# Splitting an operand one step behind its addition, and giving the chunk products of the RWKV key projection all four quarters of the TensorE array

## Chip, core and metric

The kernel runs on one core of a Trainium2 chip. The metric is the device time of one execution in microseconds (us). TensorE is PE in the views, its weight loads PEld, VectorE DVE, ScalarE ACT, GpSimd POOL, and SP the engine whose queue issues most DMAs.

## What is computed

Two decoder layers over 2048 tokens of width 1024: a sliding-window attention layer, then an RWKV-7 time-mixing layer, each followed by a gated per-layer embedding. The change touches only the RWKV layer. Cut to what matters:

```python
def rwkv7_mixer(h, mu, w_in, ...):
    xx = jnp.pad(h, ((0, 0), (1, 0), (0, 0)))[:, :-1] - h
    xs = h[None] + xx[None] * mu[:, None, None, :]          # token-shifted operands, one per projection
    proj = jnp.einsum('cbtd,dce->cbte', xs[:4], w_in.reshape(C, 4, RWKV_WIDTH))
    r, k, v, z = proj[0], proj[1], proj[2], proj[3]
    ...
    def step(S, inp):                                       # 16 heads of 64 x 64 state, 2048 steps
        sa = jnp.einsum('bhvk,bhk->bhv', S, -kk_t)
        S = S * d_t[:, :, None, :] + sa[..., None] * (kk_t * a_t)[:, :, None, :] + v_t[..., None] * k_t[:, :, None, :]
        y = jnp.einsum('bhvk,bhk->bhv', S, r_t)
        return S, y
```

The kernel does the recurrence in chunks of 64 tokens. Inside a chunk the steps are tied together by a 64 x 64 triangular matrix for each head, which has to be inverted. Its entries are products of decayed keys with each other; the projection phase computes them and leaves them in DRAM, and the recurrence phase reads them and inverts them.

## The kernel before

Four phases follow each other: `attn_proj` (to about 780 us), `attention` (to about 1215), `rwkv_proj` (to about 1960) and `rwkv` (to the end). Float32 matrices are multiplied in three passes: `split` (L531 to L540) makes a rounded high part with a ScalarE copy (L538) and a low part with a subtraction (L540, on VectorE or GpSimd), and `mm3` (L589 to L591) issues high x high, high x low, low x high. A projection tile of 128 channels x 512 tokens is 8 steps k of 3 matmuls of 128x512, 24 in all.

`rwkv_proj` computes r, then k, then v. For each it walks over 4 pairs of channel tiles and, in a pair, over 4 groups n of 512 tokens. Two kinds of generators run beside the projections, advanced by one `tick` per k step:

- `fill(c, n)` makes the operand of projection c for token group n: for each of 8 steps it loads `hp`, ScalarE scales it into `xs` (L974), VectorE adds the shifted part (L975), and `split` makes `xH` and `xL` from `xs`. `xs` has 2 buffers, `hp` 3.
- `evac_r`, `evac_k`, `evac_v` take a finished tile out of PSUM. `evac_k`, 32 times in all, is the long one: low-rank product `ls` (L1029), its tanh `lth` (L1031), squares split into `sh` and `so`, head sums `ss` (L994, L995), a VectorE transpose of `ss` (L1060), a reciprocal root on GpSimd, then the operands `kee` and `kx`, and at last the product `pab` (L1092): for each of 8 chunks and for both heads of the tile one 64x64 matmul. `pab` is copied to `kab` (L1095), two 32-row blocks are moved inside it (L1099), and it goes to DRAM.

The array's rows are the partitions that a matmul reads, its columns those that it writes. A 64x64 matmul takes a quarter of the array: head e reads partition half e, and in the kernel before writes half e, so `pab` uses two of the four quarters, and one PSUM tile.

`ls`, `ss` and `pab` share a PSUM pool `p_s` of 3 buffers, one bank each, in the order in which the program claims them; a fourth claim waits until the tile three claims back has been read. In `evac_k` there are three claims: `ls`, `ss`, `pab`. The other 5 of the 8 banks hold projection tiles.

The order on each engine is not that of the Python code. The tile framework runs a list scheduler over the recorded instructions with a timing model of its own and fixes a queue for each engine; on the chip each engine takes its queue strictly in that order and waits on semaphores.

In the last phase, `chain(c)` runs for each of 32 chunks: `r1p` (L1350), `up` (L1370, rows of one half, columns of the same half for each head), `y` (L1362) and the turned output `ytp` (L1365). `y` of head h reads and writes half h of its bank, `ytp` reads half h and writes the other half in another bank; the two are issued alternately.

## Time and profile before

| | us |
|---|---|
| median of 3 runs (3050.54 to 3063.81) | 3053.57 |
| the profiled execution | 3054.03 |
| its span, first to last instruction | 3052.3 |
| PE busy | 2828.1 (93%) |
| DVE busy | 1888.7 (62%) |
| ACT busy | 1341.6 (44%) |
| mean granted clock of TensorE | 0.965 |

A view by stage tells more than these shares: the r projection with its fills is about 1215 to 1395, the k projection with `evac_k` about 1440 to 1770, and fills for k and v lie at about 1398 to 1493 and 1654 to 1769. A wait view lists, for PE, which tile it waited to use, who released it, total us, how often, and the longest. In a timeline row stand start, duration, engine, line, operation, tiles and count; equal neighbours are merged. Matmuls overlap in the pipeline, so the cost of one is the distance of starts, not its duration. A float32 matmul of 64x64 has two records, so `pab` with its 16 matmuls is 32 records.

### The profile page before, as it was taken

To read this page: it belongs to the slowest core of one execution; us is meant where nothing else is said; L and a number is where in the kernel's file an instruction comes from. 1 tells how busy PE (TensorE), PEld (TensorE's weight loads), DVE (VectorE), ACT (ScalarE), POOL (GpSimd) and SP (SyncE) were. 2 spreads that over 40 slices of the span, in tenths; PEclk is the share of its full clock that TensorE was granted. 3 is DMA by queue.
4 is the path that set the end of the run, shared out by engine and by line. 5 is a ranking of instruction groups with operands and counts; after the bars stand their busy time and mean duration, and the time that the engine had idled before them with its cause. 6 is when DMAs were issued, how large, how long until landed. Compare 5 with 4: busy or idle time off the path is not lost. (4 is left out here: it accounts for less than half of the span.)

```text
span 3052.3 us, 56599 instructions
## 1 busy us (share of the span) xinstructions
PE 2828.1 (93%) x21416; PEld 2241.3 (73%) x21416; DVE 1888.7 (62%) x3433; ACT 1341.6 (44%) x2872; POOL 1006.4 (33%) x886
## 2 busy tenths in 40 slices
PE   7999999899999999799899899888889889889987
PEld 5888887677777777587677678666767677677866
DVE  6532434676677655747777876686684785774444
ACT  5311114784465543525768743333334344334422
POOL 2242510001221242303656610224454435435421
PEclk9999999999999999999999999999899999999999
DMA  7664857999887587636656788887879889759674
GB/s 224 189 143 104 167 146 219 285 284 337 271 257 218 196 276 253 176 128 179 199 186 206 217 218 219 243 283 190 203 195 240 219 224 253 181 164 260 186 252 159
DMA packets 625232, 652.43 MB, mean 214 GB/s; under 512 B 261696, under 2 KB 435904, under 8 KB 624960
## 3 DMA queue, kind: packets, MB, share of 16 engines
q1 hardware_dynamic: 617280, 638.32, 70.7%
q0 software_dynamic: 7680, 10.50, 3.1%
q8 instruction: 169, 2.77, 0.4%
q14 instruction: 103, 0.84, 0.1%
HBM read 421.40 MB, written 216.79 MB: 209 GB/s over the span
## 5 line engine op out<-in xcount | busy, mean ns | idle before, releaser
L589 PE MATMUL ps<-dhi,dwh 128*128 128x512 f32 x1472 | 609.0, 415 | 37.4 <-ACT dhi L538 17.7
L591 PE MATMUL ps<-dhi,dwl 128*128 128x512 f32 x1472 | 589.8, 401 | 12.8 <-DVE dwl L536 8.3
L590 PE MATMUL ps<-dlo,dwh 128*128 128x512 f32 x1472 | 592.0, 403 | 7.4 <-DVE dlo L540 4.7
L589 PE MATMUL ps<-xH,wh 128*128 128x512 f32 x1408 | 551.2, 398 | 17.1 <-ACT xH L538 11.7
L590 PE MATMUL ps<-xL,wh 128*128 128x512 f32 x1408 | 556.1, 395 | 7.4 <-DVE xL L540 4.2
L591 PE MATMUL ps<-xH,wl 128*128 128x512 f32 x1408 | 556.0, 395 | 5.5 <-DVE wl L540 5.5
L589 PEld LDWEIGHTS ps<-dhi,dwh 128*128 128x128 f32 x1472 | 281.9, 192 | 110.6 <-ACT dhi L538 20.2
L591 PEld LDWEIGHTS ps<-dhi,dwl 128*128 128x128 f32 x1472 | 282.2, 192 | 79.3 <-DVE dwl L536 9.2
L590 PEld LDWEIGHTS ps<-dlo,dwh 128*128 128x128 f32 x1472 | 282.4, 192 | 65.7 <-DVE dlo L540 6.6
L589 PEld LDWEIGHTS ps<-xH,wh 128*128 128x128 f32 x1408 | 265.1, 190 | 81.0 <-ACT xH L538 17.1
L590 PEld LDWEIGHTS ps<-xL,wh 128*128 128x128 f32 x1408 | 266.7, 189 | 70.1 <-DVE xL L540 7.2
L591 PEld LDWEIGHTS ps<-xH,wl 128*128 128x128 f32 x1408 | 266.7, 189 | 64.4 <-DVE wl L540 7.9
L699 POOL DMA_DIRECT2D t<-t x160 | 126.2, 1256 | 201.3 <-issue 79.2
L873 ACT ACTIVATE S<-S,nm 128x256 f32<-128x256 f32 (+1 forms) x256 | 125.5, 492 | 67.0 <-DVE nm L870 60.5
L540 POOL TENSOR_TENSOR xL<-xs,xH 128x512 fp32r<-128x512 f32 x72 | 103.4, 1443 | 110.0 <-ACT xH L538 104.8
L538 ACT ACTIVATE wh<-wr 128x1024 fp32r<-128x1024 f32 x44 | 46.6, 1059 | 185.3 <-DMA wr<-in_attn_w_in 151.5
L864 DVE CUSTOM_DVE_ANT_0 S<-sc,mask,sink 128x256 f32<-128x256 f32 (+1 forms) x256 | 108.8, 469 | 25.7 <-PE sc L860 25.6
L1285 DVE TENSOR_TENSOR tmp<-P 128x30 f32<-128x30 f32 (+14 forms) x240 | 111.0, 462 | 11.5 <-POOL P L1276 5.0
L975 DVE SCALAR_TENSOR_TENSOR xs<-hp,mu,xs 128x512 f32<-128x512 f32 x96 | 82.0, 861 | 47.2 <-ACT xs L974 41.6
L1287 DVE TENSOR_TENSOR P<-P,tmp 128x30 f32<-128x30 f32 (+14 forms) x240 | 105.9, 441 | 6.8
L540 POOL TENSOR_TENSOR dlo<-z,dhi 128x512 fp32r<-128x512 f32 x16 | 22.3, 1411 | 262.1 <-ACT dhi L538 255.5
L540 POOL TENSOR_TENSOR so<-sq,sh 128x512 fp32r<-128x512 f32 x32 | 45.1, 1408 | 189.2 <-ACT sh L538 123.4
(258 smaller groups left out, 5288.2 us busy)
## 6 DMA issues: line engine op xcount, KB each, us to landing
hp<-hn SPq DMA_DIRECT2D x72, 256.5 KB, 3.9
sz<-th SPq DMA_DIRECT2D x64, 256.0 KB, 4.6
ple<-pt SPq DMA_DIRECT2D x64, 256.0 KB, 6.9
aux<-ple SPq DMA_DIRECT2D x64, 256.0 KB, 4.5
yd<-kx SPq DMA_DIRECT2D x32, 512.0 KB, 4.4
dwh<-wp_ao SPq DMA_DIRECT2D x24, 512.0 KB, 4.7
dwl<-wp_ao SPq DMA_DIRECT2D x24, 512.0 KB, 6.0
dwh<-wp_ag SPq DMA_DIRECT2D x24, 512.0 KB, 4.3
```

The lines of the kernel that those rows point to most:

```text
L538: nc.scalar.activation(hi, src, AF.Copy)
L540: e.tensor_tensor(out=lo, in0=src, in1=f32(hi), op=ALU.subtract)
L589: mm(ps, lhsT=wh, rhs=ah, start=first, stop=False)
L590: mm(ps, lhsT=wh, rhs=al, start=False, stop=False)
L591: mm(ps, lhsT=wl, rhs=ah, start=False, stop=last)
L699: nc.gpsimd.dma_start(out=t1[32 * d:32 * d + 32, :], in_=t2[32 * a:32 * a + 32, :], accum_op=ALU.add)
L864: nc.vector.tensor_tensor_reduce(out=S[:, i, c0:], in0=sc[:, eo, c0:], in1=mask[:, c0:], scale=1.0, scalar=sink[:, 4 * g + 2 * j + eo:4 * ...
L873: nc.scalar.activation(S[:, i, c0:], S[:, i, c0:], AF.Exp, bias=nm[:, i:i + 1], accum_out=den[:, i:i + 1])
L975: nc.vector.scalar_tensor_tensor(out=src, in0=t[:, :G], scalar=mus[:, c, k:k + 1], in1=src, op0=ALU.mult, op1=ALU.add)
L1285: nc.vector.tensor_tensor(out=t, in0=P[:, 0:r, r:r + 1].broadcast_to([128, r, n]), in1=P[:, r:r + 1, r + 1:].broadcast_to([128, r, n]), op ...
L1287: nc.vector.tensor_tensor(out=P[:, 0:r, r + 1:], in0=P[:, 0:r, r + 1:], in1=t, op=ALU.add)
```

## The change

In `fill`, the split of step k - 1 is written ahead of the scaling and the addition of step k, where it stood behind the addition of its own step; the number of ticks per fill stays 16 at the usual pace. In `evac_k`, even chunks go to one PSUM tile and odd chunks to a second one, and in odd chunks the two heads write the opposite halves, so all four quarters of the array are addressed. `pab` now makes two claims on `p_s`, four in all for `evac_k`. The copy to `kab` becomes two copies of half the size, and the block moves read `kab` instead of PSUM. Since the halves of odd chunks are now swapped in DRAM, `chain` writes `r1p` of odd chunks into swapped halves and reads `tt` and `r1` from there; `up` of an odd chunk reads one half and writes the other.

```diff
--- before.py
+++ after.py
@@ -965,17 +965,20 @@
                     nc.sync.dma_start(out=t[:, n == 0:], in_=hn1[rows, n * G - (n > 0):n * G + G])
                     return t
 
-                ts = [load(0), load(1)]
-                for k in range(KT):
+
+                ts, src = [load(0), load(1)], None
+                for k in range(KT + 1):
                     if k + 2 < KT:
                         ts.append(load(k + 2))
                     yield
-                    t, src = ts[k], fp.tile([128, G], F32, name="xs", bufs=2)
-                    nc.scalar.activation(src, t[:, 1:], AF.Copy, scale=omu[:, c, k:k + 1])
-                    nc.vector.scalar_tensor_tensor(out=src, in0=t[:, :G], scalar=mus[:, c, k:k + 1], in1=src,
-                                                   op0=ALU.mult, op1=ALU.add)
-                    self.split(H[n, k], L[n, k], src, lo_engine="pool" if k % 4 else "dve")
-                    for _ in range(pace - 1):
+                    if k:
+                        self.split(H[n, k - 1], L[n, k - 1], src, lo_engine="pool" if k % 4 != 1 else "dve")
+                    if k < KT:
+                        t, src = ts[k], fp.tile([128, G], F32, name="xs", bufs=2)
+                        nc.scalar.activation(src, t[:, 1:], AF.Copy, scale=omu[:, c, k:k + 1])
+                        nc.vector.scalar_tensor_tensor(out=src, in0=t[:, :G], scalar=mus[:, c, k:k + 1], in1=src,
+                                                       op0=ALU.mult, op1=ALU.add)
+                    for _ in range(pace - 1 if 0 < k < KT else 0):
                         yield
 
             def proj(ps, w, n):
@@ -1086,17 +1089,20 @@
                 for _ in range(12):
                     yield
 
-                pab = p_s.tile([128, G], F32, name="pab", tag="s")
+
+                pab = [p_s.tile([128, G // 128, 64], F32, name="pab", tag="s") for _ in range(2)]
+                h = (slice(0, 64), slice(64, 128))
                 for c in range(G // 64):
-                    for h in (slice(0, 64), slice(64, 128)):
-                        nc.tensor.matmul(pab[h, c * 64:c * 64 + 64], lhsT=x[h, c, 0], rhs=ee[h, c * 64:c * 64 + 64],
+                    for e in range(2):
+                        nc.tensor.matmul(pab[c % 2][h[e ^ (c % 2)], c // 2], lhsT=x[h[e], c, 0], rhs=ee[h[e], c * 64:c * 64 + 64],
                                          start=True, stop=True)
                 ao = ring("d", "kab")
-                nc.scalar.copy(ao, pab)
+                for o in range(2):
+                    nc.scalar.copy(ao.rearrange("p (c o t) -> p o c t", o=2, t=64)[:, o], pab[o])
 
                 for e in range(2):
-                    v, u = (x[64 * e + 32:64 * e + 64].rearrange("p (c t) -> p c t", t=64) for x in (ao, pab))
-                    nc.scalar.copy(v[:, :, 0:32], u[:, :, 32:64])
+                    v = ao[64 * e + 32:64 * e + 64].rearrange("p (c t) -> p c t", t=64)
+                    nc.scalar.copy(v[:, :, 0:32], v[:, :, 32:64])
                 nc.sync.dma_start(out=ab[rc], in_=ao)
 
             def evac_v(ps, ct, n):
@@ -1347,7 +1353,7 @@
                 pairs = [(p, eo) for p in range(NP) for eo in range(2)]
                 r1p = p_c.tile([128, NP, 64], F32, name="r1p", tag="ch")
                 for p, eo in pairs:
-                    mm(r1p[half[eo], p], lhsT=am[:, p, eo, 0:LC], rhs=uv[:, eo, p], start=True, stop=True)
+                    mm(r1p[half[eo ^ c % 2], p], lhsT=am[:, p, eo, 0:LC], rhs=uv[:, eo, p], start=True, stop=True)
                 r1 = r2.tile([128, NP, 64], F32, name="r1")
                 nc.scalar.copy(r1, r1p)
                 if c + 1 < NCH:
@@ -1367,7 +1373,8 @@
                     YT[c - 1] = tp
                 up = p_c.tile([128, NP, 64], F32, name="up", tag="ch")
                 for p, eo in pairs:
-                    mm(up[half[eo], p], lhsT=tt[half[eo], p], rhs=r1[half[eo], p], start=True, stop=True)
+
+                    mm(up[half[eo], p], lhsT=tt[half[eo ^ c % 2], p], rhs=r1[half[eo ^ c % 2], p], start=True, stop=True)
                 for eo in range(2):
                     nc.scalar.copy(uv[half[eo], eo], up[half[eo]])
                 self.ticks(STEPS[1])
```

The order on ScalarE in the middle of the r projection, where the fill of token group 2 runs (L974 scales, L538 makes the high part, L1031 and L1042 belong to `evac_r`), before:

```order
L974 ACTIVATE xs<-hp,omu 128x512 x2
L538 ACTIVATE xH_11467<-xs 128x512
L538 ACTIVATE xH_11469<-xs 128x512
L974 ACTIVATE xs<-hp,omu 128x512 x2
L538 ACTIVATE xH_11471<-xs 128x512
L538 ACTIVATE xH_11473<-xs 128x512
L1042 ACTIVATE re<-lth 128x512
L974 ACTIVATE xs<-hp,omu 128x512
L1031 ACTIVATE lth<-ls,v_w_1127 128x512
```

Scalings already stood in pairs here, with the pair of high parts behind the pair of scalings. The same place in the changed kernel, where L978 is the scaling and L1034 and L1045 are the two of `evac_r`:

```order
L978 ACTIVATE xs<-hp,omu 128x512 x2
L538 ACTIVATE xH_11467<-xs 128x512
L538 ACTIVATE xH_11469<-xs 128x512
L978 ACTIVATE xs<-hp,omu 128x512 x2
L538 ACTIVATE xH_11471<-xs 128x512
L538 ACTIVATE xH_11473<-xs 128x512
L1045 ACTIVATE re<-lth 128x512
L978 ACTIVATE xs<-hp,omu 128x512
L1034 ACTIVATE lth<-ls,v_w_1127 128x512
```

Nothing moved but line numbers. The same holds for every row of every engine's queue when the `fill` edit is made alone: the queues, their waits and the tiles' places in memory stay as they were.

The order on PE in the k projection, at one `evac_k` (the eleventh), before:

```order
L590 MATMUL ps_14370<-xL32_11476,wh_13772 128x512
L591 MATMUL ps_14370<-xH32_11475,wl_13773 128x512
L1092 MATMUL pab_14296<-kee_14162,kx_14173 64x64 x16
L994 MATMUL ss_14350<-sh_14283,blk_r_1148 128x512
L995 MATMUL ss_14350<-so_14284,blk_r_1148 128x512
L589 MATMUL ps_14370<-xH33_11477,wh_13772 128x512
L590 MATMUL ps_14370<-xL33_11478,wh_13772 128x512
```

Here `pab` is one piece of 16 matmuls, followed by the head sums of a later tile. The same `evac_k` in the changed kernel (`pab_14316` takes the even chunks, `pab_14317` the odd ones):

```order
L1032 MATMUL ls_14293<-low_14051,l2h_13826 128x512
L1032 MATMUL ls_14293<-low_14051,l2l_13827 128x512
L1097 MATMUL pab_14316<-kee_14180,kx_14191 64x64 x8
L590 MATMUL ps_14392<-xL33_11478,wh_13780 128x512
L591 MATMUL ps_14392<-xH33_11477,wl_13781 128x512
L589 MATMUL ps_14392<-xH34_11479,wh_13780 128x512
L590 MATMUL ps_14392<-xL34_11480,wh_13780 128x512
L591 MATMUL ps_14392<-xH34_11479,wl_13781 128x512
L1097 MATMUL pab_14317<-kee_14180,kx_14191 64x64 x8
L589 MATMUL ps_14392<-xH35_11481,wh_13780 128x512
```

The product is cut in two pieces of 8, with five projection matmuls between; each piece uses two quarters of the array.

The order on PE at the ninth `evac_k` of the changed kernel (before, it was one piece of 16 as above):

```order
L589 MATMUL ps_14220<-xH27_11469,wh_13780 128x512
L1097 MATMUL pab_14144<-kee_14008,kx_14019 64x64 x2
L1097 MATMUL pab_14145<-kee_14008,kx_14019 64x64 x2
L1097 MATMUL pab_14144<-kee_14008,kx_14019 64x64 x2
L1097 MATMUL pab_14145<-kee_14008,kx_14019 64x64 x2
L1097 MATMUL pab_14144<-kee_14008,kx_14019 64x64 x2
L1097 MATMUL pab_14145<-kee_14008,kx_14019 64x64 x2
L1097 MATMUL pab_14144<-kee_14008,kx_14019 64x64 x2
L1097 MATMUL pab_14145<-kee_14008,kx_14019 64x64 x2
L997 MATMUL ss_14200<-sh_14131,blk_r_1148 128x512
L998 MATMUL ss_14200<-so_14132,blk_r_1148 128x512
```

Here the two tiles alternate by chunk, so four matmuls in a row stand in four quarters.

## Rows read from the trace of the kernel before

**Rows 1.** Busy time of each engine by stage of `rwkv_proj`, us:

```profile
core 0: us, PE busy (x) PEld busy (x) DVE busy (x) ACT busy (x) POOL busy (x), PEclk, DMA share, GB/s
1215.00:1395.00 180.00, 162.33 (x671) 124.59 (x670) 97.63 (x117) 71.91 (x112) 34.10 (x47) 0.99 0.49 150
1395.00:1500.00 105.00, 93.84 (x477) 73.40 (x475) 82.10 (x104) 71.84 (x122) 56.08 (x50) 1.00 0.62 181
1500.00:1650.00 150.00, 143.07 (x1074) 112.59 (x1075) 109.67 (x171) 105.70 (x189) 89.91 (x56) 0.98 0.62 202
1650.00:1775.00 125.00, 112.47 (x760) 86.72 (x759) 107.88 (x152) 100.69 (x179) 79.13 (x58) 0.96 0.73 221
```

**Rows 2.** Waits of PE, r projection, 1215 to 1395: us in total, times, longest us:

```profile
PE ps L589 <- ACT xH L538: 8.7, 7, 1.9
PE ps L590 <- DVE xL L540: 3.3, 3, 1.4
```

**Rows 3.** Waits of PE in the k projection, 1395 to 1775:

```profile
PE ss L994 <- ACT sh L538: 10.7, 7, 3.2
PE ss L995 <- DVE so L540: 6.6, 6, 3.0
PE pab L1092 <- DVE kb L1060: 0.3, 1, 0.3
```

**Rows 4.** Timeline of PE at one whole `pab`: start, us, engine, line, tiles:

```profile
1602.04 0.39 PE L590 MATMUL ps<-xL,wh 128*128 128x512 f32 x1
1602.27 0.39 PE L591 MATMUL ps<-xH,wl 128*128 128x512 f32 x1
1602.59 1.15 PE L1092 MATMUL pab<-kee,kx 64*64 64x64 f32 x32
...
1604.01 0.40 PE L995 MATMUL ss<-so,blk_r 128*128 128x512 f32 x1
```

**Rows 5.** Timeline of PE at a `pab` that another matmul cuts in two:

```profile
1594.56 0.40 PE L1029 MATMUL ls<-low,l2h 128*128 128x512 f32 x1
1594.89 0.44 PE L1092 MATMUL pab<-kee,kx 64*64 64x64 f32 x6
1595.26 0.50 PE L1029 MATMUL ls<-low,l2l 128*128 128x512 f32 x1
1595.69 1.02 PE L1092 MATMUL pab<-kee,kx 64*64 64x64 f32 x26
...
1596.98 0.39 PE L995 MATMUL ss<-so,blk_r 128*128 128x512 f32 x1
```

**Rows 6.** Timeline of PE in the last phase, `ytp` and `y` by turns:

```profile
2205.26 0.22 PE L1365 MATMUL ytp<-ident,yc 64*64 64x64 f32 x1
2205.26 0.22 PE L1362 MATMUL y<-uv,xa 64*64 64x64 f32 x1
2205.27 0.22 PE L1365 MATMUL ytp<-ident,yc 64*64 64x64 f32 x1
2205.27 0.22 PE L1362 MATMUL y<-uv,xa 64*64 64x64 f32 x1
2205.32 0.22 PE L1365 MATMUL ytp<-ident,yc 64*64 64x64 f32 x1
```

**Rows 7.** Durations of the copies of `pab`: min/median/max ns:

```profile
L1099 ACT COPY kab<-pab x64: 363/365/371, 1490.3 to 1767.7; 32x256 f32<-32x256 f32 x64
L1095 ACT COPY kab<-pab x32: 567/582/592, 1488.2 to 1764.7; 128x512 f32<-128x512 f32 x32
```

**Rows 8.** Timeline: head sums on PE and their transpose, first and last of 32:

```profile
1459.39 0.40 PE L995 MATMUL ss<-so,blk_r 128*128 128x512 f32 x1
...
1465.94 0.71 DVE L1060 STREAM_TRANSPOSE kb<-ss 128x512 f32<-128x512 f32 x1
...
1731.30 0.40 PE L995 MATMUL ss<-so,blk_r 128*128 128x512 f32 x1
...
1734.58 0.67 DVE L1060 STREAM_TRANSPOSE kb<-ss 128x512 f32<-128x512 f32 x1
```

## Prediction

> **What bounds the kernel now.** I read the stages first. In all of them PE is the busiest engine. In the r projection it works 162.3 of 180 us, in the three stretches of the k projection 93.8 of 105, 143.1 of 150 and 112.5 of 125 [rows 1]. So a microsecond of PE's work counts wherever PE does not wait, and the idle rest (17.7, 11.2, 6.9 and 12.5 us) is what better overlap could return. Then I read the waits. In the r projection PE waits for the high and low parts of the operand, 8.7 and 3.3 us [rows 2]; that is the stall at which the `fill` edit points. In the k projection it waits for the split of the squares, 10.7 and 6.6 us; for a PSUM buffer for `pab` it waits 0.3 us in 36 pieces [rows 3]. Last comes the timeline around one `pab`, because the second edit changes PE's own work there [rows 4 to 6].
>
> **Part 1, `fill`.** No instruction is added or removed. The order shown for ScalarE is the same before and after, and it is the same in every row of every queue when this edit is made alone: the list scheduler had already put two scalings ahead of two high parts. The 12.0 us of waits [rows 2] lie in queues that do not change. Cost 0, gain 0; no cover is needed, since not one DMA or wait moves.
>
> **Part 2, the array's time for `pab`.** A step of the projection is 0.227 us (1602.04 to 1602.27). From the L591 ahead of a whole `pab` to the L995 behind it 1.74 us pass; two ordinary steps take 0.45 of it, so `pab` costs 1.29 [rows 4]. In the last phase `ytp` and `y` address four quarters: four records start within 0.01 us, and the next turn begins 0.058 us later [rows 6]. `pab` has 32 records in two quarters, so 16 turns or 0.93 us; the remaining 0.35 is what entering and leaving costs. With four quarters it would be 8 turns, 0.47 us.
>
> But the gain needs the right order. I counted PE's queue of the changed kernel. Of 32 products 19 stay whole: 7 alternate between the two tiles from the first matmul (0.47 us saved each), 4 after one or two extra pairs (0.35), 2 later still (0.23), and 6 stand as eight even, then about eight odd (0.12, where the two groups overlap). That is 3.3 + 1.4 + 0.5 + 0.7 = 5.9 us. Thirteen are cut in pieces. Twelve of them are 8 and 8, nothing saved (one of these has its first matmul apart as well, 0.1 lost), one is 11 and 5 (0.35 saved). In all **6.1 us of array time go**.
>
> **Part 3, more pieces.** Before, the queue holds 36 pieces of `pab` (28 whole, 4 cut in two), now 46. Each piece pays entering and leaving again: 10 x 0.35 = **+3.5 us**. The other bound is a measured cut: 2.42 us from the L1029 ahead of it to L995, less three steps, is 1.74, against 1.29 whole, 0.45 more [rows 5]; so +4.5 at most. I take 0.35, because most pieces now stand 4 to 20 matmuls apart and not one.
>
> **Part 4, the ring of three banks.** `evac_k` now claims four buffers of three, so a `pab` tile more often has to wait until VectorE has transposed the `ss` of a later tile (L1060). Behind a waiting `pab` the whole PE queue stands: projections, `ss`, `ls`. In the queue before, 22 products wait for such a transpose, with 5.4 to 8.2 us of PE's work between that `ss` and the `pab`; now 26 tiles do, with 1.6 to 6.2 us. The transposes ended 6.9 us after their L995 at the first and 3.6 at the last of 32, on average 3.1 [rows 8]. Each of the 26 distances against each of the 32 lags gives 13.6 us of waits; the same sum for the 22 distances before gives 1.65, and there the row says 0.3 [rows 3], since a PE that waits lets VectorE catch up. A fifth of 13.6 is 2.5; I take **+3 us**. Ends: +12 (13.6 - 1.65), and -5, because the 17.3 us of waits for the squares [rows 3] are dealt out anew and could also fall by a third.
>
> **Part 5, ScalarE.** One copy of 582 ns becomes two of half the size. No copy of 128x256 from PSUM stands here; the move of 32x256 takes 365 ns [rows 7], the nearest row, with as many elements in each partition; I take that: 2 x 0.365 - 0.582 = +0.15 us, 32 times, 4.7 us of ScalarE's time. It is covered where ScalarE is busy 70% (105.7 of 150), hardly where it is busy 81% beside a fill (100.7 of 125) [rows 1] and PE waits for it. A third of the products lie there: **+1 us**, between 0 and 4.7. The two moves now read SBUF; the nearest row is their own 365 ns, so 0.
>
> **Part 6, the recurrence.** `r1p` only swaps halves: 0. `up` of the 16 odd chunks now starts in the two quarters in which the last `ytp` ran, so its first matmuls stand behind two turns: 16 x 0.117 = 1.9 us at most. PE is not always what is waited for there; **+1 us**. The scheduler also shifts single groups of three matmuls in this phase; I give that 0, with 3 us to both sides.
>
> **Sum.** 3054.0 (the profiled execution; the median of the runs is 0.5 lower) - 6.1 + 3.5 + 3 + 1 + 1 = 3056.4. What a measurement can tell from no change is about 0.5%, 15.3 us: below 3038.3 or above 3068.8. Neither edit gets near it.
>
> **Rivals.**
>
> *Ring-bound, slower.* The second tile's wait becomes the rule. PE idles 10% in the stretch where its queue is irregular (12.5 of 125) and 4.6% where it repeats (6.9 of 150) [rows 1]; now the queue is irregular throughout. If the quiet stretch goes to 10% (+8 us) and the two others idle half as much again (+12), the time is 3054.0 - 2.6 + 2 + 20 = 3073. It decides if the transpose regularly lags more than about 4.7 us, the middle of the new distances, instead of 3.1. For it: the first of the 32 lags was 6.9 [rows 8]. Against: 0.3 us of such waits so far.
>
> *Waits for the squares go, faster.* `pab`'s bank is free after copies of about 0.37 us instead of 1.31 (0.582 + 2 x 0.365 [rows 7]), so later claims come earlier and PE has other work to put ahead. Without the 17.3 us: 3054.0 - 2.6 + 2 - 17.3 = 3036. Against: those waits end with ScalarE and VectorE, whose work does not shrink.
>
> *Order does not matter, all 32 products halve.* 32 x 0.47 = 14.9 us saved, +3.5 as above with parts 4 to 6: 3047.6; with no price for the extra pieces 3044. Against: in the turns of rows 6 starts follow the queue, and PE would have to take a later odd chunk ahead of an even one. The Trainium skill ("TensorE: Matmul & The Clock Gate", Part 3) says that matmuls start and end in program order and only weight loads are pulled ahead, which is against this rival too.
>
> *Two tiles give nothing.* If two heads, from different rows, could not write one bank together, a pair of one chunk would run one after the other, and four quarters would be no faster than two: 3056.4 + 6.1 = 3062.5. Against: two of the four records that start within 0.01 us are `y` of both heads, in one bank [rows 6]. The Trainium skill ("TensorEngine Tiling (Array Packing)", Restrictions and Gotchas) states just that limit, that different row tiles cannot access the same bank at the same time; rows 6 disagree, at least for different partition halves.
>
> *The `fill` edit does act.* Then 12.0 us of waits [rows 2] could go: 3044. Against: identical queues.
>
> **How the numbers follow.** Forecast 0.69, ring-bound 0.13, squares 0.05, all halve 0.06, two tiles give nothing 0.05, `fill` acts 0.02. Predicted 3056. The range takes the forecast's bounds: down -6.1 + 3.5 - 5 - 3 is 3043.4, up -6.1 + 4.5 + 12 + 4.7 + 1.9 is 3071; all ends at once are unlikely, so 3045 to 3070. It holds the forecast, most of "halve" and "nothing", and the lower part of ring-bound. Faster by over 0.5% takes the squares and a little of the others, 0.06; slower takes most of ring-bound, 0.12; the rest, 0.82, is within 0.5%.
>
> **What would show it.** After the change, the waits for `xH` and `xL` in the r projection should stay near 12 us (part 1). Whole alternating products should take about 0.8 us between their neighbours less two steps, the cut ones 1.6 together (parts 2, 3). `pab` should show waits of 1 to 5 us in total on the transpose (part 4); over 12 means ring-bound. The two copies should take about 0.37 us each (part 5). I am wrong if the stretch from 1395 to 1775 changes by over 10 us, or if the r projection moves at all.

## The result and the profile after

The changed kernel is slower: 3079.93 us (median of 9 runs, 3068.89 to 3085.27) against 3053.26 (9 runs, 3048.35 to 3063.81); ratio 1.008, 95% interval 1.0068 to 1.0093. Forecast was 3056, between 3045 and 3070. The profiled execution of after has a span of 3076.2 us, that of before 3052.3. So the change costs 0.8%, and the time lies above the range.

Where the 23.9 us lie is read from PE's busy time in stretches that begin and end at the same work in both kernels: from the end of VectorE's last read of an r tile to the last `pab` (the k projection), from there to the first `aps`, the first product of the recurrence phase (the v projection), and from there to the last `ytp` (the recurrence). Columns: stretch, its length, PE busy (records), granted clock, DMA share, GB/s. Before:

```profile
1456.00:1760.00 304.00, 280.19 (x2012) 0.97 0.64 203
1760.00:1956.80 196.80, 187.06 (x864) 1.00 0.84 217
1956.80:2916.50 959.70, 862.76 (x11405) 0.93 0.80 218
```

After:

```profile
1454.30:1781.50 327.20, 288.89 (x2028) 0.95 0.61 193
1781.50:1971.20 189.70, 182.59 (x846) 0.99 0.82 217
1971.20:2941.20 970.00, 867.80 (x11405) 0.92 0.78 216
```

The k projection is 23.2 us longer, the v projection 7.1 shorter (part of its steps now run earlier: 16 records more in the k stretch), together +16.1. The recurrence is 10.3 longer. What comes ahead of the k projection is 1.7 us shorter, what comes behind the recurrence 0.8.

In the k projection PE idles 38.3 us instead of 23.8 (length less busy), 14.5 more. The busy time grew too, by 8.7. Of that 3.6 are the 16 steps that came over from v, at 0.227 us each. The rest is there although the product's own work shrank: the granted clock fell from 0.97 to 0.95, that is, it stood at 1.2 instead of 2.4 GHz for a larger part of the stretch. 0.03 of 304.0 and 0.05 of 327.2 are 9.1 and 16.4 us of full-speed time, so an estimate of what the clock takes is 7 us.

The stages of [rows 1] in the changed kernel, same columns:

```profile
1215.00:1395.00 180.00, 163.31 (x671) 125.42 (x670) 99.84 (x119) 72.89 (x113) 34.12 (x48) 0.98 0.49 150
1395.00:1500.00 105.00, 94.29 (x473) 74.19 (x471) 79.19 (x102) 70.35 (x120) 56.76 (x50) 0.97 0.63 184
1500.00:1650.00 150.00, 136.65 (x1041) 104.98 (x1031) 103.72 (x162) 103.10 (x197) 82.12 (x53) 0.98 0.59 190
1650.00:1775.00 125.00, 105.43 (x682) 80.52 (x683) 107.99 (x148) 100.22 (x189) 83.48 (x59) 0.90 0.66 206
```

The r projection works as before, and the first stretch of k idles as before; the loss begins in the quiet stretch from 1500, idle 13.4 instead of 6.9, and goes on in the next, 19.6 instead of 12.5.

What PE waits for in the k projection, 1395 to 1790, before (the rows that [rows 3] left out):

```profile
PE ps L589 <- DVE kb L1083: 4.4, 6, 1.5
...
PE ss L994 <- ACT kab L1099: 0.7, 2, 0.4
```

and after:

```profile
PE ps L589 <- DVE kb L1086: 18.0, 12, 4.2
PE ss L997 <- ACT kab L1101: 11.3, 6, 3.6
...
PE pab L1097 <- DVE kb L1063: 3.3, 3, 2.2
PE ss L997 <- ACT sh L538: 2.9, 2, 1.9
PE ss L998 <- DVE so L540: 2.1, 2, 1.5
```

The wait that I had priced, `pab` on the transpose, is 3.3 us, just as forecast. Two others grew. `ss` waits for a bank in which a product still lies uncopied (0.7 before, 11.3 now), and a projection waits for one of its five banks until VectorE has made `kb` (4.4 before, 18.0 now). The waits for the squares fell from 17.3 [rows 3] to 5.0.

The two belong together, as the other engines' waits in the same window show. First VectorE and GpSimd of before, then the two and ScalarE of after:

```profile
DVE kb L1060 <- PE ss L995: 2.5, 2, 2.1
...
POOL kb L1064 <- DVE kb L1063: 12.2, 9, 2.9
```

```profile
DVE kb L1063 <- PE ss L998: 10.4, 6, 3.5
...
POOL kb L1067 <- DVE kb L1066: 39.1, 17, 5.0
...
ACT kab L1101 <- PE pab L1097: 10.4, 8, 2.2
```

A late `ss` makes its transpose late, that the root on GpSimd, that `kb`; and `kb` is the last reader of the projection's bank. The starts in the two traces show this for all 32 tiles: from the last matmul of a k tile to its `ss` 15.7 us pass before and 22.0 after, to the end of `kb` 32.3 and 37.3 (means). The fifth tile behind, which needs the bank again, begins 3.5 us after `kb` before and 1.0 after, the first 30 tiles taken. But most of that delay isn't waiting. In PE's queue `ss` stands 40 projection matmuls behind its tile before and 56 after: 16 steps of 0.227 us are 3.7 of the 6.3 us. The scheduler, laying out four claims on three banks, had moved the head sums back before the kernel ran; standing there, they hardly wait for the squares any more.

One place where `ss` does wait, on the timeline of after (start, duration, engine, line; in brackets the idle time ahead and its releaser):

```profile
1546.56 0.98 PE L1097 MATMUL pab<-kee,kx 64*64 64x64 f32 x32
...
1548.23 0.80 ACT L1081 ACTIVATE kb<-lth,oka,v_k_a 128x512 f32<-128x512 f32 x1
1549.03 0.65 ACT L1101 COPY kab<-pab 128x256 f32<-128x256 f32 x2
...
1549.45 0.50 PE L997 MATMUL ss<-sh,blk_r 128*128 128x512 f32 x1 [1.91 <-ACT kab L1101]
...
1550.98 0.63 PE L590 MATMUL ps<-xL,wh 128*128 128x512 f32 x1
...
1551.41 0.63 PE L591 MATMUL ps<-xH,wl 128*128 128x512 f32 x1
```

The product is done by 1547.5, but ScalarE has other work ahead of its two copies and begins them at 1549.03. `ss` needs the bank of one of the two tiles and stands at the head of PE's queue. And after the stall the projection's steps start 0.43 us apart (1550.98, 1551.41) and not 0.23. The granted clock (the column behind the records) was at its upper level through the stall and at its lower one for much of the time behind it:

```profile
1546.00:1549.40 3.40, 1.54 (x35) 1.00 0.20 77
1551.00:1556.00 5.00, 5.00 (x18) 0.71 0.67 157
```

A stall can be paid a second time in this way. Not each one is: PE waits 1.89 us ahead of the L589 at 1599.85 too, and the steps behind that (1600.18, 1600.41) start 0.23 apart. The Trainium skill ("TensorE: Matmul & The Clock Gate", Part 1, "A second HAM failure mode: psum-queue depth-cycling") describes a kernel in which short idle gaps between matmul groups, as it cycles through PSUM banks, make the clock swing between its two levels. The place at 1549.45 agrees with it, 1.00 and then 0.71; the place at 1599.85 does not show it.

### The profile page after: what moved, and what is told of

It is laid out like the page before. It is cut to its first block, busy times and chain, and to the rows that moved or that the text cites. A ratio compares the mean times of both kernels' runs of the same rounds, so it can differ in the third digit from the quotient of the medians.

```text
span 3076.2 us, 56576 instructions
## 1 busy us (share of the span) xinstructions
PE 2838.8 (92%) x21416; PEld 2251.6 (73%) x21416; DVE 1893.0 (62%) x3433; ACT 1345.1 (44%) x2904; POOL 1008.6 (33%) x886
## 5 line engine op out<-in xcount | busy, mean ns | idle before, releaser
L589 PE MATMUL ps<-dhi,dwh 128*128 128x512 f32 x1472 | 608.9, 415 | 27.0 <-ACT dhi L538 9.6
L589 PE MATMUL ps<-xH,wh 128*128 128x512 f32 x1408 | 558.2, 403 | 31.0 <-DVE kb L1086 18.0
L590 PE MATMUL ps<-xL,wh 128*128 128x512 f32 x1408 | 563.4, 401 | 7.5 <-DVE xL L540 4.7
L591 PE MATMUL ps<-xH,wl 128*128 128x512 f32 x1408 | 562.7, 400 | 5.0 <-DVE wl L540 5.0
L589 PEld LDWEIGHTS ps<-dhi,dwh 128*128 128x128 f32 x1472 | 282.1, 192 | 99.7 <-ACT dhi L538 12.4
L589 PEld LDWEIGHTS ps<-xH,wh 128*128 128x128 f32 x1408 | 268.5, 192 | 95.6 <-DVE kb L1086 22.3
L538 ACT ACTIVATE wh<-wr 128x1024 fp32r<-128x1024 f32 x44 | 46.6, 1059 | 177.5 <-DMA wr<-in_attn_w_in 143.3
L864 DVE CUSTOM_DVE_ANT_0 S<-sc,mask,sink 128x256 f32<-128x256 f32 (+1 forms) x256 | 108.9, 470 | 22.2 <-PE sc L860 22.0
L1067 POOL TENSOR_TENSOR kb<-kb,mhalf 128x16 f32<-128x16 f32 x32 | 104.7, 3272 | 41.1 <-DVE kb L1066 39.1
L1291 DVE TENSOR_TENSOR tmp<-P 128x30 f32<-128x30 f32 (+14 forms) x240 | 109.4, 456 | 12.3 <-POOL P L1282 6.2
L264 DVE TENSOR_TENSOR aux<-ps,aux 128x512 f32<-128x512 f32 x64 | 43.8, 686 | 106.6 <-PE ps L591 97.9
```

The lines of the kernel that those rows point to most:

```text
L538: nc.scalar.activation(hi, src, AF.Copy)
L589: mm(ps, lhsT=wh, rhs=ah, start=first, stop=False)
L590: mm(ps, lhsT=wh, rhs=al, start=False, stop=False)
L591: mm(ps, lhsT=wl, rhs=ah, start=False, stop=last)
L864: nc.vector.tensor_tensor_reduce(out=S[:, i, c0:], in0=sc[:, eo, c0:], in1=mask[:, c0:], scale=1.0, scalar=sink[:, 4 * g + 2 * j + eo:4 * ...
L1067: nc.gpsimd.tensor_tensor(out=bs[:, :, 0], in0=bs[:, :, 0], in1=self.mhalf.broadcast_to([128, m]), op=ALU.pow)
```

## Experiments

Each kernel was timed beside the kernel before on the same chip; that one's medians were 3056.44 (e1 to e4), 3055.32 (e5 to e8), 3053.39 (e9 to e12) and 3055.37 (e13 to e15).

**The two other edits alone.** e1 is `fill` of the change alone. e2 is the recurrence's edit alone, so that odd chunks use the other head's matrices:

```diff
-  mm(r1p[half[eo], p], lhsT=am[:, p, eo, 0:LC], ...)
+  mm(r1p[half[eo ^ c % 2], p], lhsT=am[:, p, eo, 0:LC], ...)
-  mm(up[half[eo], p], lhsT=tt[half[eo], p], rhs=r1[half[eo], p], ...)
+  mm(up[half[eo], p], lhsT=tt[half[eo ^ c % 2], p], rhs=r1[half[eo ^ c % 2], p], ...)
```

> The kernel before with the edit of fill alone; product, PSUM claims and recurrence as before. My theory (the scheduler had already put the split one step behind, and every engine's queue is the same): the time of before within 0.2%, the r projection's waits for xH and xL at 12 us as before. Rival (the edit acts through something that the queues do not show): a change of 5 us or more, in either direction.

> The kernel before with the edit of the recurrence alone: odd chunks write r1p into swapped halves and up goes from one half to the other, while the product still leaves its halves unswapped, so odd chunks use the other head's matrices and only the time is meant. Theory A (the recurrence is slower by itself, from up running in the quarters of the last ytp or from the order that the scheduler makes of it): about 9 us slower, nothing before 1957 us changed. Theory B (the recurrence is only slower because it starts later and meets its transfers otherwise): the time of before within 3 us.

e1: 3054.05, ratio 0.9996 (0.9985 to 1.0007). e2: 3057.05, ratio 1.0009 (0.9993 to 1.0025). Neither makes the loss by itself. Left is `pab`.

**Two tiles without four quarters.** e3 has two product tiles and two copies, but both heads keep their halves, so that two quarters are used, and the recurrence is that of before. e5 has one product tile and one claim, with the two half copies and the moves out of SBUF.

```diff
 e3, against before
-  pab = p_s.tile([128, G], F32, name="pab", tag="s")
+  pab = [p_s.tile([128, G // 128, 64], F32, name="pab", tag="s") for _ in range(2)]
+  nc.tensor.matmul(pab[c % 2][h[e], c // 2], lhsT=x[h[e], c, 0], ...)
   ...                                          # copies and moves as in the changed kernel
 e5, against before
-  nc.scalar.copy(ao, pab)
+  for o in range(2):
+      nc.scalar.copy(*(x.rearrange("p (c o t) -> p o c t", o=2, t=64)[:, o] for x in (ao, pab)))
-  nc.scalar.copy(v[:, :, 0:32], u[:, :, 32:64])     # u is pab
+  nc.scalar.copy(v[:, :, 0:32], v[:, :, 32:64])
```

> The changed kernel without the swap of halves: even and odd chunks go to two PSUM tiles (four claims on three banks), two copies, but each head keeps its own half, so two quarters only and the recurrence as before. Theory ring (the claims on three banks cost the time): the k projection 1395 to 1785 as slow as in the changed kernel or up to 6 us slower, since the array gain is gone, so about 3068 to 3075 in all. Theory quarters (four quarters at once disturb each other): the k projection back at the time of before, 3053 to 3057 in all.

> The kernel before with one product tile, one claim and 64x64 products in two quarters, but copied out in two halves of 128x256 and with the two block moves reading SBUF: ScalarE's part of the change and nothing else. Theory A (the fourth claim on three banks makes the loss): within 0.3% of the kernel before, 3045 to 3062; idle of PE between the last r tile and the last product stays near the 23.8 us of before. Theory B (the second copy delays ScalarE's queue and so everything behind it): at least a third of the loss, 3062 or more, idle over 30 us.

e3: 3080.84, ratio 1.0086 (1.0064 to 1.0108), so the loss is there without any change of quarters; it is even above the 3068 to 3075 expected. e5: 3049.18, ratio 0.9981 (0.9967 to 0.9994): ScalarE's part costs nothing, it even gains a little (it holds the earlier release of the bank that e6, below, has alone). Between the two stands the second tile, with the order that the scheduler makes of it: 1.0086 / 0.9981 = 1.0105. In the profiled executions that is 21.8 us of the k and v projections and 7.2 of the recurrence (table below). PE's waits of e3 from 1395 to 1790 have the pattern of after:

```profile
PE ps L589 <- DVE kb L1083: 14.4, 9, 4.7
PE ss L994 <- ACT kab L1098: 4.7, 4, 2.1
...
PE pab L1094 <- DVE kb L1060: 3.8, 3, 1.8
```

**The claim or the hold.** e8 is the kernel before with a fourth tile that is written once and read by nobody:

```diff
+  pad = p_s.tile([128, 64], F32, name="pad", tag="s")
+  nc.tensor.matmul(pad, lhsT=ee[:, 0:128], rhs=x[:, 0, 0], start=True, stop=True)
   pab = p_s.tile([128, G], F32, name="pab", tag="s")
```

> The kernel before with one more tile claimed from the ring of three banks ahead of each product; it gets one matmul of 128x64 (32 in all, estimated 0.1 us each, 3 us together) and is read by nobody. Copies, moves and the product are as before. Theory A (the number of claims, through the order that it gives to the ring, is enough): 3068 or more, idle of PE in the k projection over 33 us. Theory B (it takes the longer hold of the second tile until its copy, not the claim as such): 3050 to 3062, idle under 28 us.

3061.15, ratio 1.002 (1.0007 to 1.0034), some 6 us. Its 32 matmuls cost more than the 0.1 us each that I had estimated:

```profile
1566.16 0.40 PE L590 MATMUL ps<-xL,wh 128*128 128x512 f32 x1
1566.40 0.33 PE L1090 MATMUL pad<-kx,kee 128*128 128x64 f32 x2
...
1566.86 0.40 PE L589 MATMUL ps<-xH,wh 128*128 128x512 f32 x1
```

0.70 us less two steps is 0.25, and 32 times that is 8 us, no less than all that e8 loses. A claim that is given back at once costs nothing that can be seen; it is the tile that waits for its copy.

**When the bank comes free.** e6 is the kernel before with only the last line of e5's edit, so that the bank is free after the copy and not after copy and two moves.

> The kernel before, only the two block moves read the copied tile in SBUF and not the product in PSUM, so that the bank is free after one copy of about 0.58 us instead of copy and two moves (about 1.31 us). Theory A (banks of the ring are what the stage is short of): a small gain, 3044 to 3052. Theory B (the ring of three is no limit with three claims): no difference, 3050 to 3058.

3048.35, ratio 0.9972 (0.996 to 0.9984): the lowest time of this study, though not clearly apart from e5. With three claims on three banks an earlier release is still worth 7 us (3055.32 - 3048.35) (not all of it in the k projection, table below).

**More banks in the ring.** e4 is the changed kernel, e7 the kernel before, with four banks for projections and four in the ring instead of five and three:

```diff
-  p_m = self.pool(left, "rp_m", 5, PSUM, side="right")
+  p_m = self.pool(left, "rp_m", 4, PSUM, side="right")
-  p_s = self.pool(left, "rp_s", 3, PSUM)
+  p_s = self.pool(left, "rp_s", 4, PSUM)
```

> The changed kernel with four banks for the ring of ls, ss and the product, and four instead of five for projection tiles. In its queue nearly all products alternate between the two tiles and stand whole. Theory ring: the k projection ends at or ahead of before, some 12 us of array time less than before and no waits of ss for a copy of the product; with the recurrence as in the changed kernel 3045 to 3060 in all. Rival (the fifth projection bank was needed, or the copies are what costs): 3070 or more, PE waiting for projection tiles to be read.

> The kernel before with four banks for projection tiles and four in the ring instead of five and three. It is the control of the changed kernel with the same banks (3077.3). Theory A (the fifth projection bank is needed by the long way out of a k tile): 3068 or more, longer v projection (over 200 us from the last product to the first aps, before 196.7). Theory B (four and four are as good, and the changed kernel loses through claims and copies whatever the banks): within 0.3% of before, 3045 to 3062.

e4: 3077.29, ratio 1.007 (1.0054 to 1.0087); my simple reading, that a fourth bank cures it, missed. e7 tells why: 3086.81, ratio 1.0096 (1.0077 to 1.0116). The fifth projection bank is itself worth 1%. PE's waits of e7 and of e4 in the k projection:

```profile
PE ps L589 <- DVE kb L1083: 17.9, 10, 5.9
```

```profile
PE ps L589 <- DVE kb L1086: 12.6, 6, 4.3
...
PE ls L1032 <- ACT kab L1101: 6.3, 4, 1.8
...
PE ss L997 <- ACT kab L1101: 0.6, 1, 0.6
```

In e4 `ss` hardly waits for the copy any more (0.6 instead of 11.3). Where each of four tiles has a bank, the changed product loses nothing: e4 is not slower than e7, and its k and v projections are 12.7 us shorter (table below), about what the array should give.

**The second tile outside the ring.** e9 puts the odd chunks into the bank of the tile's own projection, which is free once `kb` has been made; three claims again, four quarters. e10 is e9 with a pause of 6 steps instead of 12 ahead of the product, e11 is e5 with that pause, e12 the changed kernel with it:

```diff
 e9, against after
-  pab = [p_s.tile([128, G // 128, 64], F32, name="pab", tag="s") for _ in range(2)]
+  pab = [p_s.tile([128, G // 128, 64], F32, name="pab", tag="s"),
+         ps[:, 0:G // 2].rearrange("p (c t) -> p c t", t=64)]
 e10 to e12
-  for _ in range(12):
+  for _ in range(6):
       yield
```

> The changed kernel, only the tile of the odd chunks lies in the bank of the key tile's own projection, which nobody reads any more once kb has been made, so that there are three claims on three banks again and all four quarters are used. Theory A (a held fourth claim on three banks made the loss): the loss is gone, 3040 to 3058. Theory B (projection banks are as short: with four of them the kernel before lost 1%): the bank is held through the pause of 12 steps, waits of projections for a bank over 20 us, 3070 or more.

> As the one with the odd chunks in the projection's own bank, with a pause of 6 steps and not 12 ahead of the product, so that that bank is held shorter. Theory A: 3036 to 3050; against the kernel before with half copies (3049) up to 32 x 0.45 = 14 us of array time less. Theory B: still 3062 or more, with projections that wait for a bank.

> Control for the two others with a pause of 6: the kernel before with half copies and one claim, two quarters, and a pause of 6 steps. Theory A (the pause alone does little): 3044 to 3056, so that what the four-quarter kernel with the same pause is below it is the array's. Theory B (a shorter pause alone is worth as much): 3036 to 3044.

> The changed kernel (four claims on three banks) with a pause of 6 steps and not 12; the scheduler then leaves all 32 products in one piece each. Theory A (the held fourth claim is the cause): still slow, 3066 to 3090, with waits of ss or ls for the product's copy and of projections for kb. Theory B (the cut products and their irregular order are the cause): 3056 or less.

e9: 3062.91, ratio 1.0031 (1.0015 to 1.0048), between the two ranges expected. Six tenths of the loss are gone; in the profiled execution only 2.9 of the 16.1 us of the k and v projections are left, the rest lies in the recurrence. Against e5, which has the same copies in two quarters, these projections are still 9.3 us longer; the projection's bank is now held longer. e10: 3079.66, ratio 1.0076 (1.0046 to 1.0106), far from the 3036 to 3050 of my theory and as its rival said: projections wait 18.1 us for `kab`, which now ends the hold of their bank, and the products wait 14.1 us for `kx`, which they now follow closely. The shorter pause spoils the other two much more, and there neither theory's range held: e11 3195.47, ratio 1.0453 (1.0427 to 1.0478), and e12 3174.1, ratio 1.0381 (1.0351 to 1.0412). In e11 the projections wait:

```profile
PE ps L589 <- DVE kb L1083: 113.5, 30, 8.5
```

The queue has `ss` 67 projection matmuls behind its tile where e5 has 34, so `kb` ends 56.0 us behind the tile and not 29.2. Why the scheduler lays it out so with six steps less was not taken further, and e12, whose queue is laid out alike, says nothing on the fourth claim. But e11 and e12 hold all 32 products in one piece, in two quarters and in four, with the same waits (113.5 and 108.6 us on `kb`), so they price the array. Their k projections, e11 and then e12:

```profile
1457.10:1900.50 443.40, 327.70 (x2022) 0.86 0.44 140
```

```profile
1458.80:1886.50 427.70, 311.72 (x2011) 0.84 0.45 144
```

15.7 us less, and 16.0 less busy time, for 32 products; forecast were 0.47 each, 14.9 in all. The stretch of e11 holds 11 records more; over k and v together, where the rest of the work is the same, it is 16.4. The granted clock was low in both, 0.86 and 0.84, so the agreement is a rough one.

**Shortage or order.** One ring also forces an order on the claims. In e13 to e15 each kind of tile of the k projection has a bank of its own instead (`ls` of the r projection and `vtp` of the v projection take turns among them); e13 is e5 so arranged, with its one tile under `tag="p"`, e14 and e15 are the changed kernel with the odd tile in the bank of `ls` or in that of `ss`:

```diff
-  ss = p_s.tile([128, G], F32, name="ss", tag="s")
+  ss = p_s.tile([128, G], F32, name="ss", tag="q")
-  lp = p_s.tile([128, G], F32, name="ls", tag="s")
+  lp = p_s.tile([128, G], F32, name="ls", tag="l" if j else "lqp"[(4 * ct + n) % 3])
-  pab = [p_s.tile([128, G // 128, 64], F32, name="pab", tag="s") for _ in range(2)]
+  pab = [p_s.tile([128, G // 128, 64], F32, name="pab", tag=t) for t in "pl"]    # e15: "pq"
-  tp = p_s.tile([128, G], F32, name="vtp", tag="s")
+  tp = p_s.tile([128, G], F32, name="vtp", tag="pl"[n % 2])
-  p_s = self.pool(left, "rp_s", 3, PSUM)
+  p_s = self.pool(left, "rp_s", 1, PSUM)
```

> Control: the kernel before with half copies (one claim, two quarters), but ls, ss and pab each keep a bank of their own in place of one ring through all three, so that a claim waits only for the tile of its own kind. Theory A (in the kernel before each claim already meets its own kind, three claims back): as with the ring, 3043 to 3060. Theory B (the order of claims that a ring forces is what costs): 3040 or less.

> The changed kernel (four quarters, two product tiles) with a bank for each kind in place of the ring; the tile of the odd chunks shares the bank of ls. Theory A (four live tiles do not fit on three banks, whatever their order): 3063 or more, with PE waiting for the read of ls or for the product's copy. Theory B (the ring's order is the cause: four claims on three banks make every claim meet another kind): the loss goes, 3035 to 3055.

> As the one whose odd tile shares the bank of ls, but it shares that of ss, so that the next head sums wait for the copy of the product and the product for the transpose of the sums. Theory A: 3063 or more, with ss waiting for kab. Theory B: 3035 to 3058.

e13: 3062.52, ratio 1.0022 (1.0013 to 1.0032), just above the range expected and 0.4% above e5: with three claims, going without the ring's order gains nothing. e14: 3097.55, ratio 1.0138 (1.0122 to 1.0155). e15: 3125.24, ratio 1.022 (1.0198 to 1.0242). Against their control they lose 1.2% and 2.0%. So it is not the order that a ring forces: four tiles, each held until its reader comes, did not fit on three banks in any of the three arrangements tried (after, e14, e15). e15 shows it in the wait that it was built for, beside the ones of after:

```profile
PE ps L589 <- DVE kb L1086: 14.9, 12, 3.3
PE pab L1097 <- DVE kb L1063: 12.6, 10, 2.8
PE ss L997 <- ACT kab L1101: 9.3, 5, 4.2
```

All stretches in one table, worked out as for before and after: k and v projection together, PE's idle time in the k projection, and the recurrence. The last two columns are means over the 32 k tiles: how many projection matmuls stand in PE's queue between the last one of a tile and its `ss`, and the time from that last one to the end of `kb`. In e4 and e7 projections have four banks and not five; in e9 and e10 a projection's bank is held beyond `kb`.

| kernel | ratio | k + v, us | idle in k, us | recurrence, us | `ss` behind its tile, matmuls | `kb` behind its tile, us |
|---|---|---|---|---|---|---|
| before | | 500.8 | 23.8 | 959.7 | 40 | 32.3 |
| after | 1.008 | 516.9 | 38.3 | 970.0 | 56 | 37.3 |
| e1 `fill` alone | 0.9996 | 499.3 | 23.1 | 961.3 | 40 | 32.3 |
| e2 recurrence alone | 1.0009 | 497.8 | 23.0 | 966.6 | 40 | 32.2 |
| e3 two tiles, two quarters | 1.0086 | 516.2 | 28.4 | 973.8 | 59 | 37.4 |
| e4 after, four banks | 1.007 | 510.7 | 36.3 | 971.7 | 29 | 28.0 |
| e5 half copies, one tile | 0.9981 | 494.4 | 17.7 | 966.6 | 34 | 29.2 |
| e6 moves from SBUF | 0.9972 | 496.3 | 17.9 | 957.4 | 38 | 30.4 |
| e7 before, four banks | 1.0096 | 523.4 | 30.1 | 971.8 | 29 | 27.7 |
| e8 claim not held | 1.002 | 508.2 | 26.6 | 962.1 | 46 | 33.6 |
| e9 odd tile in own projection's bank | 1.0031 | 503.7 | 26.5 | 967.9 | 28 | 27.1 |
| e10 the same, pause 6 | 1.0076 | 512.7 | 41.9 | 969.9 | 47 | 35.6 |
| e11 e5, pause 6 | 1.0453 | 634.2 | 115.7 | 969.4 | 67 | 56.0 |
| e12 after, pause 6 | 1.0381 | 617.8 | 115.9 | 962.0 | 66 | 54.5 |
| e13 e5, a bank for each kind | 1.0022 | 509.6 | 22.2 | 966.0 | 37 | 29.1 |
| e14 after, odd tile with `ls` | 1.0138 | 536.8 | 30.4 | 963.4 | 53 | 38.3 |
| e15 after, odd tile with `ss` | 1.022 | 562.4 | 47.2 | 967.6 | 64 | 41.4 |

Wherever a second tile is held on the three banks (after, e3, e14, e15), `ss` stands 53 to 64 matmuls behind its tile and `kb` ends 37 to 41 us behind it. With one tile and a pause of 12 (before, e1, e2, e5, e6, e13) it is 34 to 40 and 29 to 32.

## Why the prediction was wrong

**What bounds the kernel: right.** The waits of PE in the k projection decide, and a microsecond lost there reaches the end. The sign that I had set for this, the stretch from 1395 to 1775 changed by over 10 us, came: the last `pab` ends 21.5 us later.

**Part 1, `fill`: right.** Waits for `xH` and `xL` in the r projection, after, against 8.7 and 3.3 [rows 2]:

```profile
PE ps L589 <- ACT xH L538: 7.6, 7, 1.7
PE ps L590 <- DVE xL L540: 3.7, 3, 1.4
```

11.3 in place of 12.0, and e1 times as before.

**Parts 2 and 3, array time: right.** One whole alternating product of after, to lay beside [rows 4]:

```profile
1556.88 0.39 PE L589 MATMUL ps<-xH,wh 128*128 128x512 f32 x1
1557.20 0.69 PE L1097 MATMUL pab<-kee,kx 64*64 64x64 f32 x32
1557.83 0.50 PE L997 MATMUL ss<-sh,blk_r 128*128 128x512 f32 x1
1558.16 0.39 PE L998 MATMUL ss<-so,blk_r 128*128 128x512 f32 x1
```

From the L589 to the L998 1.28 us, less two steps 0.83; forecast 0.8, before 1.29. That the rest of 0.35 is paid by every piece also holds, as one half of a cut product shows:

```profile
1590.36 0.39 PE L589 MATMUL ps<-xH,wh 128*128 128x512 f32 x1
1590.68 0.68 PE L1097 MATMUL pab<-kee,kx 64*64 64x64 f32 x16
...
1591.63 0.39 PE L998 MATMUL ss<-so,blk_r 128*128 128x512 f32 x1
```

A piece of 16 records costs 1.27 less two steps, 0.82, two of them 1.64 (forecast 1.6). The rival "two tiles give nothing" is out: 0.69 in place of 1.15 for 32 records, although both heads, from different rows of the array, write one bank. The Trainium skill ("TensorEngine Tiling (Array Packing)", Restrictions and Gotchas) excludes that; for different partition halves the trace disagrees, by these 0.69 us. "All 32 halve" is out as well, since 13 products stay cut, as counted from the queue.

**Part 5, ScalarE: right.** The copies, after, by minimum, median and maximum in ns:

```profile
L1101 ACT COPY kab<-pab x64: 347/372/396, 1486.5 to 1784.0; 128x256 f32<-128x256 f32 x64
L1105 ACT COPY kab<-kab x64: 400/403/409, 1488.2 to 1785.4; 32x256 f32<-32x256 f32 x64
```

0.372 us against 0.365 taken. The moves out of SBUF take 38 ns longer than those out of PSUM [rows 7], which I gave 0; 64 of them are 2.4 us. e5, with all of that, loses nothing, and it times like e6, which has the moves alone.

**Part 4, the ring: here the sum failed.** It had +3, at most +12. Parts 2 to 5 together had +1.4; the k and v projections took +16.1. The mechanism, banks of the ring, was named, and the wait of `pab` for the transpose came out as forecast (3.3). The error is that I priced the ring by the new claimant's wait alone. The second tile also holds a bank, from the first matmul of the product until ScalarE comes to the copy, and that was priced at nothing. The `ss` behind it stands 16 matmuls further back in the queue and waits 11.3 us besides, `kb` comes 5.0 us later by it, and projections wait 13.6 us more for their banks. I had the copies under part 5 only as work, not as the end of a hold, and the five projection banks not at all, though before they had little slack: 3.5 us between `kb` and the next use of its bank, and e7 shows that one fewer costs 1%. The place of `ss` stood in the queue that I had counted for `pab`, and the prediction doesn't have it. The other term that was missing is the clock, about 7 us by the estimate above.

The rival "ring-bound", 3073, named the right resource, and one of its measures nearly fits: in the quiet stretch 13.4 of 150 us are idle, 8.9%, where it said 10%. That its time came near is partly luck: what it described, the second tile's own wait becoming the rule, did not happen, the first stretch of k idles no more than before (10.7 us, 11.2 before), and the clock and the recurrence were not in it. Its point of decision was wrong. The transposes lag no more than before (from the start of the L995 or L998 to their end 3.5 us on average before, 3.1 after); it decides at the copies and in the place of `ss`. So was the sign that I set: "over 12 on `pab` means ring-bound" would have read 3.3 as not bound. The 17.3 us for the squares did fall, by 12.3, as the rival "waits for the squares go" wanted, and it helped nothing, because `ss` now stands behind other work and other waits.

**Part 6, the recurrence: +10.3 in place of +1, with 3 to both sides.** It isn't the exchange of halves: e2 has it and times as before, and e3, without it, has the longest recurrence of all, 973.8. Over the kernels it lies between 957.4 and 973.8, with no order by its start; the eight that have the exchange have a mean of 967.4, the nine that don't 965.3. So about 2 us go with the exchange, and before and after happen to lie on opposite sides. A term of about 8 to both sides would have been right. (The range's upper end was also added up without the 3 us of this part: 3074, not 3071, and then cut to 3070.) Whether the scheduler's other order there makes it, or one execution differs so much from another, stays open; e1, with the same queues as before, differs by 1.6.

What is shown: the second tile, held on three banks, makes the loss of the k and v projections (e3 against e5, e14 and e15 against e13), not the copies (e5), the bare claim (e8) or the four quarters (e4 against e7, e12 against e11). Shown by the traces too is the way that it takes, `ss` late and with it `kb` and the projections' banks, and that the larger part of the delay stands in the queue. Not shown is how much of the loss would remain on the chip if the scheduler kept the order of before, since every variant also gave it another one. Open is the recurrence, 10.3 of the 23.9 us.

## What to carry to other kernels

A new tile in a ring of PSUM banks is priced by its hold: from its first write until its reader's engine, in queue order, comes to it. Lay that beside the holds of all tiles on the ring, and follow the wait of whoever meets it through to the next pool. Where a scheduler lays out the queue ahead of time, part of the price is paid there: count how far the other claimants have moved back (here `ss` from 40 to 56 matmuls) before trusting the waits of the old trace. To shorten a hold (here reading the copy instead of the bank, 0.9972) can be worth more than to halve the array time of the work in it.

## What was not expected of the hardware

- With 14.5 us more of idle time in the k projection the granted clock fell from 0.97 to 0.95, by an estimate 7 us; behind one of the stalls steps lie 0.43 us apart instead of 0.23, behind another they don't.
- A float32 matmul of 128x64, two records, cost 0.25 us between projection matmuls (e8), more than a projection step of 128x512 at 0.227.
- A ScalarE move of 32x256 took 403 ns out of SBUF and 365 out of PSUM.
